# Strassen-like blocks of the down projection: weight sums made in place, and by adding DMAs in two blocks

## The chip, the cores and the metric

One NeuronCore of a Trainium2 chip runs the kernel. The metric is the device time of one execution in microseconds (us), median of 3 runs.

## The reference, cut to what matters

One layer of a diffusion transformer on 256 tokens of width 2048. After attention and a first layer norm, the feed-forward part and the second norm end the layer:

```python
def swiglu(u, w_gate, w_up, w_down):
    return (jax.nn.silu(u @ w_gate) * (u @ w_up)) @ w_down

x = layer_norm(DN_ALPHA * x + g1 * (heads @ w_out[layer]), ln1_g[layer], ln1_b[layer])
x = layer_norm(DN_ALPHA * x + g2 * swiglu(modulate(x, sh2, sc2), w_gate[layer], w_up[layer], w_down[layer]),
               ln2_g[layer], ln2_b[layer])
```

All is float32. Call `h = silu(u @ w_gate) * (u @ w_up)`, 256 x 5632; the change concerns only `h @ w_down`, with `w_down` 5632 x 2048.

## The kernel before, in words

**Precision.** TensorE multiplies float32r numbers. Each float32 operand is split into a rounded part (hi) and the rest (lo), and one product of tiles is three matmuls: hi·hi, lo·hi, hi·lo (`mm3`, L242 to L244). For a weight tile of 128 x 1024, ScalarE casts hi (L232 in `split_raw`, L238 in `split`) and VectorE subtracts to get lo (L233, L239). Four hi and four lo tiles rotate (`HL_BUFS = 4`), so ScalarE and VectorE can be at most four tiles ahead of TensorE.

**The down projection.** The rows of `w_down` are 11 groups f of 512, its columns 4 blocks n of 512, done as two pairs of column blocks (n = 0, 1 and n = 2, 3). For one f and one n, `plain` loads a 512 x 512 piece (1 MB, SP's queue, L210), splits it into two tiles and runs 24 matmuls, all four 128-row chunks for the first 128 tokens and then for the other 128. In a pair, the word "f3" of this text is group 3 with the pair's first column block, "s3" group 3 with its second.

**By quarters.** For some groups (8, 9, 10 in the first pair, 7 to 10 in the second) `by_quarters` does both column blocks of the pair at once. It takes h as 2 x 2 (tokens by row halves) and the weights as 2 x 2 (b11, b12 in one loaded 1 MB tile, b21, b22 in another), and needs 7 products of 6 matmuls in place of 8. Their names, in order: p1, b, a, p7, p5, p6, c. Four of the seven right-hand sides are sums of weights, which VectorE makes with four 128 x 1024 additions (L1780): two into the extra tile `room["x"]` (names x1, x2; "sums" in the trace), two in place. Each product then splits its right side into one hi and one lo tile. Products p1, p5, p6, p7 are collected in four PSUM banks of their own and put together once per pair (`combine_parts`, L1815 to L1820).

The left sums s1 to s4 of a group are made beforehand: `quarter_sums` for 8 to 10 in the first pair, and `late_quarter_sums` for 7, which writes them over quarters of h that nothing reads any more. The one in group 7's own tile can only be written when "s7" is done.

**The order.** Before, the words of the first pair are f0 f1 8 f2 f3 9 f4 f5 f6 f7 s0 10 s1 C s2 s3 A s4 Q s5 s6 s7 R, of the second f0 f1 E 7 f2 8 f3 9 f4 10 f5 f6 s0 C L N s1 A s2, then the last four groups of the last block together. C combines the products, A and E finish a column block (gate, residual, norm statistics), Q and R are the late sums, L loads the rows of the last norm, N makes rows of it (a memset and small DMAs on GpSimd's queue, L1739 and L1741, and an activation on ScalarE, L1743). This part lies outside the hand-ordered regions: a planner lays out each engine's instructions at build time, the program's order being the priority, and an instruction that is not ready by its reckoning can be passed by a later one. Each engine and each queue then runs in that order.

**Raw tiles.** Four 1 MB tiles (`RAW_BUFS = 4`) rotate for the loads. A group by quarters holds two until its last product is split.

Of the kernel before, what the change touches and what calls it, by code (L numbers as in the profile page):

```python
# [16 lines left out]
AF = mybir.ActivationFunctionType  # L17
# [148 lines left out]
def dit_layer(ctx: ExitStack, tc: tile.TileContext, x, c, cx, c_ctx, w_ada, b_ada, w_in, q_norm_g,  # L166
# [37 lines left out]
    def raw_tile():  # L204
        return wraw.tile([P, G4 * NB], F32, tag="raw", name="raw")

    def load_raw(w, k0, nk, c0, width):
        raw = raw_tile()
# [1278 lines left out]
    def quarter_sums(f, hf):  # L1487
        i = list(QUARTERS).index(f)
        if i == 0:
            both = pb.tile([P, 2, 2, 4, 2, P], F32R, tag="u2h", name="quarters")  # L1490
            room["q"] = [both[:, 0], both[:, 1], pb.tile([P, 2, 4, 2, P], F32R, tag="u2l0", name="quarters")]
            room["x"] = pb.tile([P, 2, 2 * NB], F32, tag="u2l1", name="sums")
        hl = [room["q"][i][:, c] for c in range(2)]
        quarters[f] = [[p[:, c] for c in range(4)] for p in hl]
        sums = room["x"][:, 0].rearrange("p (s q t) -> p s q t", s=4, q=2)
        s1, s2, s3, s4 = (sums[:, c].rearrange("p q (a i) -> p q a i", a=4) for c in range(4))
        (a11, a12), (a21, a22) = ([hf[t].rearrange("p (a q i) -> p q a i", a=4, q=Q)[:, k : k + 2] for k in (0, 2)]
                                  for t in range(NT))
        for o, x0, x1, op in ((s1, a21, a22, ALU.add), (s2, s1, a11, ALU.subtract), (s3, a11, a21, ALU.subtract),
                              (s4, a12, s2, ALU.subtract)):  # L1500
            nc.vector.tensor_tensor(o, x0, x1, op=op)
        split(*hl, sums)

    def late_quarter_sums(f):
        whole, sums = (room["x"][:, i] for i in range(2))
        nc.vector.tensor_add(whole, hTh[f].rearrange("p q t -> p (q t)").bitcast(F32), hTl[f].rearrange("p q t -> p (q t)").bitcast(F32))
        whole = whole.rearrange("p (q t) -> p q t", q=4)
        (a11, a12), (a21, a22) = ([whole[:, k : k + 2, t * P : (t + 1) * P] for k in (0, 2)] for t in range(NT))
        sums = sums.rearrange("p (s q t) -> p s q t", s=4, q=2)
        s1, s2, s3, s4 = (sums[:, c] for c in range(4))  # L1510
        quarters[f] = [[c[g][:, 0:2, P:] for g in (f, *QUARTERS)] for c in (hTh, hTl)]
        for o, x0, x1, op in ((s1, a21, a22, ALU.add), (s2, s1, a11, ALU.subtract), (s3, a11, a21, ALU.subtract),
                              (s4, a12, s2, ALU.subtract)):
            nc.vector.tensor_tensor(o, x0, x1, op=op)
# [244 lines left out]
    def by_quarters(f, n, bank, begins, ends, last):
        r1, r2 = (load_raw(w_down, f * 4 + k, 2, n * NB, 2 * NB).rearrange("p (k n) -> p k n", k=2) for k in (0, 2))  # L1760
        (b11, b12), (b21, b22) = ([r[:, :, :NB], r[:, :, NB:]] for r in (r1, r2))
        x1, x2 = (room["x"][:, i].rearrange("p (k n) -> p k n", k=2) for i in range(2))
        h = [(c[f][:, 0:2, :P], c[f][:, 2:4, :P], c[f][:, 2:4, P:]) for c in (hTh, hTl)]
        q = quarters[f]
        lefts = {n: [h[c][i] for c in range(2)] for i, n in enumerate(("a11", "a12", "a22"))}
        lefts.update({f"s{i + 1}": [q[c][i] for c in range(2)] for i in range(4)})
        sub, add = ALU.subtract, ALU.add
        for name, left, right, after in (
            ("p1", "a11", b11, (x1, b22, b12, sub)),
            ("b", "s4", b22, (b12, b12, b11, sub)),  # L1770
            ("a", "a12", b21, (x2, x1, b11, add)),
            ("p7", "s3", x1, (b21, b21, x2, sub)),
            ("p5", "s1", b12, None),
            ("p6", "s2", x2, None),
            ("c", "a22", b21, None),
        ):
# [4 lines left out]
            own = len(name) == 2  # L1781
            for j in range(2):
                mm3(bank(name), lefts[left][0][:, j], lefts[left][1][:, j], (hi[:, j], lo[:, j]),
                    j == 0 and begins(name), j == 1 and (ends if own else last and name != "b"))
        turn()
        turn()

    def pair(n, order, by_parts, left=0):
        banks, begun, held = {}, set(), {}

        def bank(name):
# [9 lines left out]
        whole = [f for f in order if f not in by_parts]
        parts = [f for f in order if f in by_parts]

        def first(f):
            if f in by_parts:
                return lambda: by_quarters(f, n, bank, begins, f == parts[-1], f == order[-1])
            return lambda: plain(f, n, (bank("a"), bank("c")), begins("a") | begins("c"), f == order[-1])

        def second(f):
            return lambda: plain(f, n + 1, (bank("b"), bank("d")), False, f == whole[-1 - left])  # L1810
# [32 lines left out]
    one = pair(0, ORDER, tuple(QUARTERS))
    run(one[0][:-1])
    second_start(0, 1, one[5])
    run(one[0][-1:])
    run(one[1][1:2])
    one[2]()
    run(one[1][2:4])
    one[3]()  # L1850
    run(one[1][4:5])
    rest = late_quarter_sums(LATE_F)
    run(one[1][5:])
    rest()
    two = pair(2, LATE_ORDER, (LATE_F, *QUARTERS), 1)
    run(two[0][:2])
    one[4]()
    run(two[0][2:])
    second_start(0, 3, two[5])
    two[2]()  # L1860
    l2_loads()
    rows_of_last_norm()
    run(two[1][1:2])
    two[3]()
    run(two[1][2:-4])
# [3 lines left out]
    fs = two[6][-4:]  # L1869
# [92 lines left out]
```

## Time and profile before

| | |
|---|---|
| median of 3 runs | 1114.36 us (1113.22 to 1115.82) |
| the profiled execution | 1114.99 us, span 1113.2 us |
| TensorE matmul busy | 1099.1 us |
| VectorE, ScalarE, GpSimd busy | 911.0, 606.9, 46.2 us |
| mean granted TensorE clock | 0.997 of full speed |

The down projection runs from about 870 us to the end. The difference of execution and span lies around the program. A matmul row lasts some 0.39 us, but the matmuls are pipelined: what counts is the distance from one start to the next. In a row of the timeline, a bracket at the end is the idle time before it and what ended it.

### The profile page before, as it was taken

The numbers are of one execution on the slowest core, as the hardware profiler recorded it, in microseconds if no ns is written. First come the engines' busy times: TensorE is split into PE (matmuls) and PEld (weight loads), VectorE is DVE, ScalarE is ACT, GpSimd is POOL, SyncE is SP. The second block draws the span as 40 slices with busy tenths as digits, with TensorE's granted clock in tenths as the row PEclk, the third lists the DMA queues.
The fourth block names the chain that finished last, engine by engine and source line by source line (L and its number), as shares of the span: only waits on it lengthen the run. The fifth ranks groups of instructions, "written<-read, shape, count | busy, mean of one in ns | idle before, by whom it ended". The sixth has DMA issues, their size and how long they took to land.

```text
span 1113.2 us, 13937 instructions
## 1 busy us (share of the span) xinstructions
PE 1099.1 (99%) x5132; PEld 887.0 (80%) x5132; DVE 911.0 (82%) x1098; ACT 606.9 (55%) x875; POOL 46.2 (4%) x94
## 2 busy tenths in 40 slices
PE   8999999999999999999999999999999999999997
PEld 6677788778888778888888888888888778888786
DVE  2469999999999898877666776887875897979996
ACT  3345675786775356444465455655654564446640
POOL 1000050102000010000000000000000000000000
PEclk9999999999999999999999999999999999999999
DMA  9999998889999789989768798898996564646562
GB/s 346 380 400 390 394 335 323 301 274 313 328 313 374 278 311 359 335 293 344 265 208 279 274 339 293 296 316 277 325 322 219 163 249 155 241 175 227 200 254 76
DMA packets 174954, 321.26 MB, mean 289 GB/s; under 512 B 9091, under 2 KB 46883, under 8 KB 172581
## 3 DMA queue, kind: packets, MB, share of 16 engines
q1 hardware_dynamic: 173206, 319.23, 81.6%
q10 hardware_dynamic: 1264, 1.11, 0.3%
q8 instruction: 40, 0.66, 0.2%
q14 instruction: 28, 0.23, 0.1%
q0 software_dynamic: 416, 0.04, 0.0%
HBM read 304.09 MB, written 16.25 MB: 288 GB/s over the span
## 4 chain that ended last, share of the span: by engine, by line
PE 91%; DVE 5%; DMA 3%; ACT 1%; issue 0%; POOL 0%; DVEq 0%; SPq 0%; ACTq 0%
PE acc L242 21%; PE acc L244 21%; PE acc L243 21%; PE wk L243 7%; PE wk L244 7%; PE wk L242 7%; PE wk L1038 2%; PE wk L560 2%; DVE lo L239 2%; DMA raw<-in_w_down_dram 1%; DMA raw<-in_w_ada_dram 1%; DVE raw L1780 1%; PE wk L730 1%; DVE sums L1780 1%; DMA adav<-in_b_ada_dram 0%; DMA rows<-in_ln_g_dram 0%
## 5 line engine op out<-in xcount | busy, mean ns | idle before, releaser
L233 DVE TENSOR_TENSOR lo<-raw,hi 128x1024 fp32r<-128x1024 f32 x228 | 275.4, 1220 | 116.7 <-ACT hi L232 114.3
L232 ACT CAST hi<-raw 128x1024 fp32r<-128x1024 f32 x228 | 239.4, 1055 | 237.1 <-PE acc L244 123.8
L242 PE MATMUL acc<-hi,u2h 128*128 128x512 f32 x448 | 175.1, 391 | 0.0
L244 PE MATMUL acc<-hi,u2l 128*128 128x512 f32 x448 | 174.5, 390 | 0.4 <-DVE u2l L1596 0.4
L243 PE MATMUL acc<-lo,u2h 128*128 128x512 f32 x448 | 174.5, 389 | 0.0
L361 DVE SCALAR_TENSOR_TENSOR adav<-raw,cs,adav 128x1024 f32<-128x1024 f32 (+1 forms) x96 | 114.4, 1191 | 7.2 <-DMA raw<-in_w_ada_dram 3.7
L509 ACT CAST hi<-raw 128x1024 fp32r<-128x1024 f32 x84 | 87.9, 1052 | 54.8 <-PE acc L244 35.8
L512 DVE TENSOR_TENSOR lo<-raw,hi 128x1024 fp32r<-128x1024 f32 x84 | 101.3, 1220 | 9.8 <-ACT hi L509 9.5
L242 PE MATMUL acc<-hi,uh 128*128 128x512 f32 x256 | 102.8, 402 | 0.3 <-ACT uh L743 0.3
L244 PE MATMUL acc<-hi,ul 128*128 128x512 f32 x256 | 100.3, 392 | 0.0
L243 PE MATMUL acc<-lo,uh 128*128 128x512 f32 x256 | 99.8, 390 | 0.0
L244 PE MATMUL wk<-hi,u2l 128*128 128x512 f32 x256 | 99.6, 389 | 0.0
L243 PE MATMUL wk<-lo,u2h 128*128 128x512 f32 x256 | 99.6, 389 | 0.0
L242 PE MATMUL wk<-hi,u2h 128*128 128x512 f32 x256 | 99.6, 389 | 0.0
L242 PE MATMUL acc<-hi,hTh 128*128 128x512 f32 x254 | 98.8, 389 | 0.6 <-ACT hi L238 0.6
L243 PE MATMUL acc<-lo,hTh 128*128 128x512 f32 x254 | 98.8, 389 | 0.0
L244 PE MATMUL acc<-hi,hTl 128*128 128x512 f32 x254 | 98.7, 389 | 0.0
L244 PEld LDWEIGHTS acc<-hi,u2l 128*128 128x128 f32 x448 | 84.1, 188 | 18.3 <-DVE u2l L1596 0.9
L242 PEld LDWEIGHTS acc<-hi,u2h 128*128 128x128 f32 x448 | 84.1, 188 | 18.2 <-ACT u2h L1595 0.8
L243 PEld LDWEIGHTS acc<-lo,u2h 128*128 128x128 f32 x448 | 84.1, 188 | 17.7 <-DVE lo L233 0.4
L242 PEld LDWEIGHTS acc<-hi,uh 128*128 128x128 f32 x256 | 48.1, 188 | 16.1 <-ACT acc L524 2.5
L244 PEld LDWEIGHTS acc<-hi,ul 128*128 128x128 f32 x256 | 48.0, 188 | 11.3 <-DVE ul L746 1.1
(328 smaller groups left out, 1786.1 us busy)
## 6 DMA issues: line engine op xcount, KB each, us to landing
raw<-in_w_ada_dram SPq DMA_DIRECT2D x64, 1024.0 KB, 7.5
raw<-in_w_gate_dram SPq DMA_DIRECT2D x44, 1024.0 KB, 6.4
raw<-in_w_up_dram SPq DMA_DIRECT2D x44, 1024.0 KB, 5.7
raw<-in_w_down_dram SPq DMA_DIRECT2D x44, 1024.0 KB, 5.2
raw<-in_w_ada_dram SPq DMA_DIRECT2D x64, 512.0 KB, 6.3
raw<-in_w_in_dram SPq DMA_DIRECT2D x18, 1024.0 KB, 7.8
raw<-in_w_out_dram SPq DMA_DIRECT2D x16, 1024.0 KB, 6.3
pd<-hx SPq DMA_DIRECT2D x64, 128.0 KB, 5.0
```

What stands on the lines that cost most here:

```text
L232: nc.scalar.copy(hi[:, :n], raw[:, s : s + n])
L233: nc.vector.tensor_tensor(lo[:, :n], raw[:, s : s + n], hi[:, :n].bitcast(F32), op=ALU.subtract)
L239: nc.vector.tensor_tensor(lo, src, hi.bitcast(F32), op=ALU.subtract)
L242: nc.tensor.matmul(ps, lhsT=xh, rhs=w[0], start=first, stop=False, skip_group_check=seeded)
L243: nc.tensor.matmul(ps, lhsT=xh, rhs=w[1], start=False, stop=False, skip_group_check=seeded)
L244: nc.tensor.matmul(ps, lhsT=xl, rhs=w[0], start=False, stop=last, skip_group_check=seeded)
L361: nc.vector.scalar_tensor_tensor(a[:, c : c + piece], raw[:, f : f + piece], cs[:, 4 * (g * (G4 * NB // w) + j) + 2, None], a[:, c : c + p ...
L509: nc.scalar.copy(hl.hi[:, :n], raw.t[:, s : s + n])
L512: nc.vector.tensor_tensor(hl.lo[:, :n], raw.t[:, s : s + n], hl.hi[:, :n].bitcast(F32), op=ALU.subtract)
L560: nc.tensor.matmul(bank.t[32 * j : 32 * j + 32, :width], lhsT=cs[:, 4 * k + 2 - 2 * i : 4 * k + 34 - 2 * i], rhs=raw.t[:, c * width : (c + ...
L1038: nc.tensor.matmul(o_ps.t[:, : 2 * P].rearrange("p (g q) -> p g q", q=32), lhsT=v, rhs=pv[:, k], start=k == 0, stop=k == 3)
L1780: nc.vector.tensor_tensor(after[0], after[1], after[2], op=after[3])
```

## The change

Weight sums no longer use `room["x"]`: all four are made in place, with other signs (b22 += b12, b12 += b11, b11 += b22, b21 += b11), each after the product that reads the old content has split it. The left sums change their signs accordingly, and so do the copy of p1 and one subtraction in `first_block`.

In the second pair the groups 7 and 9 are taken apart into three words each: "a" (loads, p1, b, a, p7, p5), "b" (p6), "c" (product c). In these two groups the last two sums (b11 += b22, b21 += b11; 512 KB each, as 128 partitions of two runs of 2 KB) are made by DMAs from SBUF to SBUF with addition, issued on GpSimd's queue. Groups 8 and 10 of that pair, and all of the first, keep four additions on VectorE.

The four raw tiles are held by hand in the second pair: two are kept for 7 and then 9, the other two and the freed `room["x"]` rotate for all other loads. "s7" moves to the head of the first pair's second half, and R ahead of s6.

```diff
-ORDER = (0, 1, 8, 2, 3, 9, 4, 5, 6, 7, 10)
-LATE_ORDER = (0, 1, 7, 2, 8, 3, 9, 4, 10, 5, 6)
+FIRST_PAIR = "f0 f1 8 f2 f3 9 f4 f5 f6 f7 s7 10 s0 s1 C s2 s3 A s4 Q s5 R s6"
+SECOND_PAIR = "f0 f1 E 7a f2 8 7b f3 7c f4 f5 9a 10 9b f6 9c s0 C L N s1 A s2"
...
+        def product(word, name, left, right):
             hi, lo = (whl.tile([P, SUB * NB], F32R, tag=tag, name=tag).rearrange("p (k n) -> p k n", k=2) for tag in ("hi", "lo"))
-            split(hi, lo, right)
-            if after:
-                nc.vector.tensor_tensor(after[0], after[1], after[2], op=after[3])
+            split(hi, lo, st[right])
...
+        def put_on(right, other):
+            nc.vector.tensor_add(st[right], st[right], st[other])
+
+        def put_apart(right, other):
+            nc.gpsimd.dma_start(st[right], st[other], accum_op=ALU.add)
+
+        last_sum = put_apart if apart else put_on
+
+        def one(word):
+            loads()
+            product(word, "p1", "a11", "b11")
+            product(word, "b", "s4", "b22")
+            put_on("b22", "b12")
+            product(word, "a", "a12", "b21")
+            put_on("b12", "b11")
+            if apart:
+                last_sum("b11", "b22")
+                last_sum("b21", "b11")
+            product(word, "p7", "s3", "b22")
+            if not apart:
+                last_sum("b11", "b22")
+            product(word, "p5", "s1", "b12")
+            if not apart:
+                last_sum("b21", "b11")
+            turn()
+
+        def two(word):
+            product(word, "p6", "s2", "b11")
+
+        def three(word):
+            product(word, "c", "a22", "b21")
+            turn()
...
-            nc.scalar.copy(c1, banks["p1"])
+            nc.scalar.activation(c1, banks["p1"], AF.Copy, scale=-1.0)
...
+    kept = [raw_tile() for _ in range(4)]
+    room["kept"], room["rooms"] = kept[:2], kept[2:] + [room["x"].rearrange("p i n -> p (i n)")]
```

## Rows read from the trace of the kernel before

**Rows 1.** The page: busy time, share of the span and instructions of the engines.

```profile
PE 1099.1 (99%) x5132; PEld 887.0 (80%) x5132; DVE 911.0 (82%) x1098; ACT 606.9 (55%) x875; POOL 46.2 (4%) x94
```

**Rows 2.** The page: the chain that ended last, shares of the span by engine.

```profile
PE 91%; DVE 5%; DMA 3%; ACT 1%; issue 0%; POOL 0%; DVEq 0%; SPq 0%; ACTq 0%
```

**Rows 3.** Windows: stretch, its length, then busy (count) of PE, PEld, DVE, ACT, POOL, clock, DMA share, GB/s.

```profile
860.00:980.00 120.00, 119.04 (x522) 97.27 (x521) 101.93 (x113) 62.31 (x65) 0.00 (x0) 1.00 0.59 204
980.00:1060.00 80.00, 79.39 (x350) 65.09 (x349) 74.93 (x72) 47.38 (x48) 4.40 (x8) 1.00 0.57 200
```

**Rows 4.** Timeline of PE: start, length, engine, line, operation, out<-in.

```profile
885.81 0.40 PE L243 MATMUL wk<-lo,quarters 128*128 128x512 f32 x1
...
887.74 0.50 PE L242 MATMUL acc<-hi,hTh 128*128 128x512 f32 x1 [0.61 <-ACT hi L238]
...
908.81 0.50 PE L243 MATMUL wk<-lo,quarters 128*128 128x512 f32 x1 [0.29 <-DVE lo L239]
...
1041.79 0.39 PE L244 MATMUL acc<-hi,hTl 128*128 128x512 f32 x1
...
1043.38 0.39 PE L242 MATMUL wk<-hi,hTh 128*128 128x512 f32 x1
...
1049.09 0.40 PE L242 MATMUL wk<-hi,quarters 128*128 128x512 f32 x1
1050.10 0.50 PE L243 MATMUL wk<-lo,quarters 128*128 128x512 f32 x1 [0.61 <-DVE lo L239]
1050.44 0.40 PE L244 MATMUL wk<-hi,quarters 128*128 128x512 f32 x1
```

**Rows 5.** Timeline of DVE around block 10 of the second pair.

```profile
1037.82 1.22 DVE L1745 SCALAR_TENSOR_TENSOR rows<-rows 1x1024 fp32r<-1x1024 f32 x1
1039.06 1.23 DVE L239 TENSOR_TENSOR lo<-raw,hi 128x1024 fp32r<-128x1024 f32 x1
1040.20 1.22 DVE L1780 TENSOR_TENSOR sums<-raw 128x1024 f32<-128x1024 f32 x1
...
1046.55 1.23 DVE L239 TENSOR_TENSOR lo<-sums,hi 128x1024 fp32r<-128x1024 f32 x1 [0.59 <-ACT hi L238]
...
1048.83 1.22 DVE L239 TENSOR_TENSOR lo<-raw,hi 128x1024 fp32r<-128x1024 f32 x1
```

**Rows 6.** Timeline of ACT: casts beside plain groups, and in block 10 of the second pair.

```profile
953.82 1.06 ACT L232 CAST hi<-raw 128x1024 fp32r<-128x1024 f32 x1 [3.02 <-PE acc L244]
955.18 1.06 ACT L232 CAST hi<-raw 128x1024 fp32r<-128x1024 f32 x1 [0.30 <-PE acc L244]
959.26 1.06 ACT L232 CAST hi<-raw 128x1024 fp32r<-128x1024 f32 x1 [3.02 <-PE acc L244]
...
1038.61 1.05 ACT L238 CAST hi<-raw 128x1024 fp32r<-128x1024 f32 x1 [0.77 <-DMA raw<-in_w_down_dram]
1042.22 1.06 ACT L238 CAST hi<-raw 128x1024 fp32r<-128x1024 f32 x1 [2.56 <-PE acc L244]
1044.95 0.63 ACT L1743 ACTIVATE rows<-rows 65x512 fp32r<-65x512 f32 x1 [1.68 <-DMA rows<-in_ln_g_dram]
```

**Rows 7.** Timeline of DVE ahead of block 10 of the first pair: sums made early.

```profile
926.24 1.23 DVE L1780 TENSOR_TENSOR sums<-raw 128x1024 f32<-128x1024 f32 x1
...
928.65 1.22 DVE L1780 TENSOR_TENSOR sums<-sums,raw 128x1024 f32<-128x1024 f32 x1
```

**Rows 8.** DMA issues by line: out<-in queue, count, KB each, median us to landing.

```profile
raw<-in_w_down_dram SPq DMA_DIRECT2D x44, 1024.0 KB, 5.2
raw<-in_w_ada_dram SPq DMA_DIRECT2D x64, 512.0 KB, 6.3
...
spill<-hd SPq DMA_DIRECT2D x20, 256.0 KB, 8.1
...
rows<-in_ln_g_dram POOLq DMA_DIRECT2D x3, 4.0 KB, 5.0
```

**Rows 9.** Timeline of GpSimd in the second pair: the only DMAs it issues there.

```profile
1039.03 1.44 POOL L1741 DMA_DIRECT2D rows<-in_ln_g_dram  x3 [0.29 <-POOL rows L1739]
```

More of the change, by code (lines that the diff above doesn't have):

```diff
@@ L205, in raw_tile, with load_raw @@
         return wraw.tile([P, G4 * NB], F32, tag="raw", name="raw")
-    def load_raw(w, k0, nk, c0, width):
-        raw = raw_tile()
+    def load_raw(w, k0, nk, c0, width, raw=None):
+        raw = raw_tile() if raw is None else raw
         rv = raw[:, : nk * width]
@@ L1498, in quarter_sums @@
                                   for t in range(NT))
-        for o, x0, x1, op in ((s1, a21, a22, ALU.add), (s2, s1, a11, ALU.subtract), (s3, a11, a21, ALU.subtract),
-                              (s4, a12, s2, ALU.subtract)):
-            nc.vector.tensor_tensor(o, x0, x1, op=op)
+        for o, x0, x1 in ((s1, a21, a22), (s2, a11, s1), (s3, a21, a11), (s4, a12, s2)):
+            nc.vector.tensor_sub(o, x0, x1)
         split(*hl, sums)
@@ L1511, in late_quarter_sums @@
         quarters[f] = [[c[g][:, 0:2, P:] for g in (f, *QUARTERS)] for c in (hTh, hTl)]
-        for o, x0, x1, op in ((s1, a21, a22, ALU.add), (s2, s1, a11, ALU.subtract), (s3, a11, a21, ALU.subtract),
-                              (s4, a12, s2, ALU.subtract)):
-            nc.vector.tensor_tensor(o, x0, x1, op=op)
+        for o, x0, x1 in ((s1, a21, a22), (s2, a11, s1), (s3, a21, a11), (s4, a12, s2)):
+            nc.vector.tensor_sub(o, x0, x1)
         def put_in(i):
@@ L1751, in mms, with plain_room @@
             mm3(ps, hTh[f][:, j, tt], hTl[f][:, j, tt], w[j], first and j == 0, last and j == 3)
+    def plain_room():
+        if "rooms" not in room:
+            return None
+        room["rooms"].append(room["rooms"].pop(0))
+        return room["rooms"][-1]
     def plain(f, n, accs, begins, ends):
-        w = load_split(w_down, f * 4, n * NB)
+        w = split_raw(load_raw(w_down, f * 4, G4, n * NB, NB, plain_room()))
         for t in range(NT):
-            mms(f, w, t, accs[t], begins, ends)
+            mms(f, w, t, accs[t], begins, ends[t] if isinstance(ends, tuple) else ends)
@@ L1757, in plain, with by_quarters, loads @@
         turn()
[L1759 to L1776, printed above, removed]
+    def by_quarters(f, n, bank, begins, closes, apart):
+        st = {}
+        def loads():
+            rooms = room["kept"] if apart else [plain_room(), plain_room()]
+            r1, r2 = (load_raw(w_down, f * 4 + k, 2, n * NB, 2 * NB, r).rearrange("p (k n) -> p k n", k=2)
+                      for k, r in zip((0, 2), rooms))
+            for i, r in enumerate((r1, r2)):
+                for j in range(2):
+                    st[f"b{i + 1}{j + 1}"] = r[:, :, j * NB : (j + 1) * NB]
+            h = [(c[f][:, 0:2, :P], c[f][:, 2:4, :P], c[f][:, 2:4, P:]) for c in (hTh, hTl)]
+            st.update({a: [h[c][i] for c in range(2)] for i, a in enumerate(("a11", "a12", "a22"))})
+            st.update({f"s{i + 1}": [quarters[f][c][i] for c in range(2)] for i in range(4)})
+        def product(word, name, left, right):
@@ L1777, in by_quarters @@
             hi, lo = (whl.tile([P, SUB * NB], F32R, tag=tag, name=tag).rearrange("p (k n) -> p k n", k=2) for tag in ("hi", "lo"))
-            split(hi, lo, right)
-            if after:
-                nc.vector.tensor_tensor(after[0], after[1], after[2], op=after[3])
-            own = len(name) == 2
+            split(hi, lo, st[right])
             for j in range(2):
-                mm3(bank(name), lefts[left][0][:, j], lefts[left][1][:, j], (hi[:, j], lo[:, j]),
-                    j == 0 and begins(name), j == 1 and (ends if own else last and name != "b"))
@@ L1785, in by_quarters @@
-        turn()
-        turn()
-    def pair(n, order, by_parts, left=0):
+                mm3(bank(name), st[left][0][:, j], st[left][1][:, j], (hi[:, j], lo[:, j]),
+                    j == 0 and begins(name), j == 1 and closes(word, name))
+        def put_on(right, other):
[3 more added lines that the diff above has]
+        last_sum = put_apart if apart else put_on
@@ L1789, in pair @@
+        def two(word):
[3 more added lines that the diff above has]
+            turn()
+        return one, two, three
+    def pair(n, words, left=0):
         banks, begun, held = {}, set(), {}
@@ L1799, in begins, with used, closes, step @@
             return fresh
[L1801 to L1810, printed above, removed]
+        words = words.split()
+        seconds = [int(w[1:]) for w in words if w[0] == "s"]
+        uses = {"f": ("a", "c"), "s": (), "1": ("p1", "b", "a", "p7", "p5"), "2": ("p6",), "3": ("c",)}
+        def used(word):
+            if word[0] in uses and not word[0].isdigit():
+                return uses[word[0]]
+            if not word[0].isdigit():
+                return ()
+            kind = {"a": "1", "b": "2", "c": "3"}.get(word[-1], "123")
+            return tuple(b for k in kind for b in uses[k])
+        last = {b: w for w in words for b in used(w)}
+        def closes(word, name):
+            return name != "b" and last[name] == word
+        def step(word):
+            if word[0] == "f":
+                f = int(word[1:])
+                return lambda: plain(f, n, (bank("a"), bank("c")), begins("a") | begins("c"), tuple(last[b] == word for b in "ac"))
+            if word[0] == "s":
+                f = int(word[1:])
+                if f == seconds[0]:
+                    return lambda: second_start(f, n + 1, bank)
+                return lambda: plain(f, n + 1, (bank("b"), bank("d")), False, f == seconds[-1] and not left)
+            if word[0].isdigit():
+                f = int(word.rstrip("abc"))
+                if f not in parted:
+                    parted[f] = by_quarters(f, n, bank, begins, closes, word[-1] == "a")
+                one, two, three = parted[f]
+                return lambda: [q(word) for q in {"a": (one,), "b": (two,), "c": (three,)}.get(word[-1], (one, two, three))]
+            return {"C": combine_parts, "A": first_block}[word]
+        parted = {}
         def combine_parts():
@@ L1825, in first_block @@
                 y = held[t]
-                nc.vector.tensor_add(y, banks["ac"[t]], y)
+                nc.vector.tensor_sub(y, banks["ac"[t]], y)
                 gated(t, n, y, y)
@@ L1833, in second_block @@
                 spread(t, n + 1)
-        return [first(f) for f in order], [second(f) for f in whole], combine_parts, first_block, second_block, bank, whole
+        return [step(w) if w not in extra else extra[w] for w in words], second_block, bank
     def second_start(f, n, bank):
-        w = load_split(w_down, f * 4, n * NB)
+        w = split_raw(load_raw(w_down, f * 4, G4, n * NB, NB, plain_room()))
         mms(f, w, 0, bank("b"), False, False)
@@ L1841, in second_start @@
         turn()
[L1843 to L1865, printed above, removed]
+    rest = []
+    extra = {
+        "Q": lambda: rest.append(late_quarter_sums(LATE_F)),
+        "R": lambda: rest[0](),
+        "L": l2_loads,
+        "N": rows_of_last_norm,
+    }
+    one, one_end, _ = pair(0, FIRST_PAIR)
+    run(one)
+    kept = [raw_tile() for _ in range(4)]
+    room["kept"], room["rooms"] = kept[:2], kept[2:] + [room["x"].rearrange("p i n -> p (i n)")]
+    extra["E"] = one_end
+    two, _, two_bank = pair(2, SECOND_PAIR, 1)
+    run(two)
     wide = pb.tile([P, 2, 2, SUB * NB], F32R, tag="u2h", name="wide")
@@ L1868, in dit_layer @@
     cols = [slice(n * NB, (n + 1) * NB) for n in range(4)]
-    fs = two[6][-4:]
+    fs = LAST_F
     ws = [load_split(w_down, f * 4, 3 * NB, rooms=() if i else wide) for i, f in enumerate(fs[:3])]
@@ L1878, in dit_layer @@
         for f, w in zip(fs[:3], ws):
-            mms(f, w, t, two[5]("bd"[t]), False, f == fs[2])
+            mms(f, w, t, two_bank("bd"[t]), False, f == fs[2])
         mms(fs[3], ws[3], t, ends[t], True, True)
@@ L1890, in dit_layer @@
             nc.vector.tensor_mul(scaled[n], xt[:, 1, cols[n]], l2g[:, cols[n]])
-        gated(0, 3, two[5]("b"), t2k("yt"))
+        gated(0, 3, two_bank("b"), t2k("yt"))
         nc.vector.tensor_add(xt[:, 0, cols[3]], xt[:, 0, cols[3]], ends[0])
@@ L1894, in dit_layer @@
         ending(0)
-        gated(1, 3, two[5]("d"), t2k("yt"))
+        gated(1, 3, two_bank("d"), t2k("yt"))
         nc.vector.tensor_add(xt[:, 1, cols[3]], xt[:, 1, cols[3]], ends[1])
```

1 line of the change is left out of this document (added).

## The prediction

> **What bounds the kernel now.** I read the page's engine line first: TensorE is busy 1099.1 of 1113.2 us [rows 1], and the chain that ended last runs on it for 91% of the span [rows 2]. The windows of the down projection show the second candidate: from 980 to 1060 VectorE is busy 74.9 of 80 us, at full clock [rows 3]. Because matmuls overlap in the pipeline, busy time hides small losses, so I then read the starts in the timeline of TensorE. From 1041.79 to 1043.38 there are seven steps: 0.227 us each [rows 4]. So a product (6 matmuls) takes 1.36, a plain group (24) 5.45, a whole block by quarters (42) 9.53 us. Between 860 and 1103 eleven starts come over 0.06 us later than this pitch, the first at 885.81, the last at 1050.44 [rows 4]. Together they lose 3.16 us: 1.47 in or just behind block 8 and 0.56 in block 9 of the first pair, 1.13 in block 10 of the second. The matmuls stay 1:1 the same, so 3.16 us is all that the change can win, and what VectorE saves counts only there.
>
> VectorE starts an operation of 1024 columns every 1.14 us (1039.06 to 1040.20) [rows 5]. A block by quarters costs it seven lo subtractions and four sums, 11 x 1.14 = 12.5 us against TensorE's 9.5. A plain group gives back 5.45 - 2 x 1.14 = 3.2. So block and plain in turn are just balanced: 14.8 against 15.0.
>
> How far VectorE may run ahead is set by the four hi and lo tiles. Beside plain groups the casts lie 1.36 apart, then 4.08 [rows 6]: a plain group's first tile is free after three quarters of it, its second at its end. Call B the moment when a block's first matmul starts (1043.38 in block 10 [rows 4]). Behind a plain group the cast of p1 may start at about B-6.5, of b at B-5.1, of a at B-1.1 (1042.22 [rows 6]), of p7 at B+0.3, then one every 1.36.
>
> **The change part by part.**
>
> *Additions that leave VectorE.* Two in block 7 and two in 9 of the second pair: 4 x 1.14 = 4.6 us. With TensorE as the bound this is worth only stall that it removes. Block 10's stall before is lo of p5, which ended at 1048.83 + 1.22 = 1050.05, and TensorE went on at 1050.10 [rows 4, 5]. In front of it stood an operation for the last norm's row (1.22 us) and a wait of 0.59 behind ScalarE's wait for that row's DMA [rows 5, 6]. N's second row now hangs on 9c and falls beside plain groups. So these 1.13 us go: -1.1.
>
> *Sums in place, the block behind a plain group.* Before, a sum into x could be made before any tile was free (926.24 to 928.65, some 12 us ahead of its products [rows 7]). In place, each sum must wait until the old content is split. By the cast times above, VectorE ends p1 at B-4.2, b at -2.8, two sums at -1.7 and -0.5, a at 1.3, p7 2.6, a sum 3.8, p5 4.9, a sum 6.0, p6 7.2, c 8.3. TensorE wants lo one matmul into each product: p7 at 4.3, p5 5.7, p6 7.0, c 8.4. So p6 is late by 0.2. That is +0.2 for block 8 of the second pair and +0.2 for block 10 of the first, which had no stall. Blocks 8 and 9 of the first pair begin with VectorE or their load late; eleven operations from the same start end at the same time, so 0.
>
> *9a straight ahead of 10.* This is the new squeeze. 9a has no plain group behind it; block 10's tiles become free one product at a time. With S the start of 9a, B = S+6.8. The cast of p1 may start only when 9's b is through: B-3.8; b B-2.4, a B-1.1. VectorE then ends p1 at B-1.5, b -0.1, sum 1.0, a 2.2, sum 3.3, p7 4.5, sum 5.6, p5 6.7, sum 7.9, p6 9.0, c 10.2. Against the same wants p7 is late by 0.2, p5 by 1.1 in all, p6 by 2.0, c by no more. The last operation alone gives 10.2 - 8.4 = 1.8 as the least; a planner that holds sums back behind the splits changes little. What could hide it is a longer lead, and four tiles allow none. +2.0. After 7a comes f2, so block 8 is spared.
>
> *The adding DMAs.* The trace shows none. For 9, the second sum on VectorE is done by about S-1, so the first DMA can start there; b's split needs the tile free at S+12.3 and is wanted at S+16.3. The second DMA needs the first landed, and 9c is wanted at S+6.8+9.5+1.4+5.4 = S+23.1. With X per DMA and 2.3 for cast and lo, 9c is in time while -1 + 2X + 2.3 is below 23.1: X up to 10.9. 7 has more room (f3 starts later): X up to 13.6. Bounds of X: 5.0, the landing of 4 KB that GpSimd issues; above, 2 x 8.1 = 16.2, the slowest small transfer with DRAM taken twice because an add also reads its target. I take 6.3, a 512 KB load with the same bytes [rows 8]; the chain of two is then 12.6 and costs 0. Both ends stay for the range. The Trainium skill ("DMA: Bandwidth & Descriptors", Anatomy of one DMA) prices such a DMA at 2.0 us plus bytes at 436 GB/s, by estimate 3.2 us here; no row shows it, and by it the chain would never be late. Traffic: 2 MB of adds in some 90 us beside DMA engines busy 57% [rows 3]. Loads have five rooms instead of four, and today's waits for them are short (0.77 [rows 6]): 0, at worst +1.
>
> *GpSimd's queue.* Issuing three small DMAs took 1.44 us [rows 9] and nothing urgent stands there: the adds of 9 and the memsets and DMAs of N, needed only in the last norm. 0.
>
> *Rest.* Copy of p1 with a scale, subtraction for addition: same operations. s7 first and R earlier end a wait that was off the path. The rooms: k0, k1 for block 9 are free when 7c is split, some 16 us ahead of 9a, against 5.2 us for a load [rows 8]. 0.
>
> Sum: -1.1 + 0.2 + 0.2 + 2.0 = +1.3 us. Against the profiled execution, 1114.99, that is 1116.3; it stands 0.6 above the median, 1114.36, so for a median I say 1115.6.
>
> **The rivals.**
>
> *The squeeze does not form.* The planner may order block 10's sums, casts and matmuls so that 9b or f6 fills the gap, or the model above is too strict by one tile. Then -1.1 +0.4 at most remains: 1113.3; and if the freer in-place sums also end the first pair's 2.0, 1111.2. For it: 4.6 us less work on VectorE. Against: eleven operations per block stay in 8 and 10 and in the whole first pair.
>
> *The adds come late (slower).* One mechanism: the chain of two DMAs of block 9 ends behind the moment when 9c wants it, ScalarE waits there in order, and s0's casts behind it. It decides from X = 10.9. At X = 12.6 (6.3 twice) it costs 2 x 1.7 = 3.4: 1119.0. At 16.2 it costs 10.6, and 7c 5.2 more: 1131. For it: GpSimd's 4 KB take 5.0 already, and the add reads twice. Against: 512 KB loads at 6.3.
>
> *The issue is held up.* VectorE is without a pause through 9a and 10, some 17 us. If GpSimd could not write its descriptors then, the chain of 9 would start at S+16 and 9c be late by about 6 us net of the squeeze: 1121. Against: the three issues at 1039.03 took 1.44 us while VectorE ran back to back [rows 5, 9]. The Trainium skill ("SBUF — State Buffer", Summary) says that descriptor writing starves while VectorE is in a doubled mode; 1024 columns in 1.14 us are no doubled rate, so by that rule and the trace it should not.
>
> *It does what it says and nothing shows:* the saved additions lie off the path, squeeze of 0.5 to 1: 1114.4. This I count with the forecast.
>
> **How the numbers follow.** 0.2% is 2.2 us: about what a measurement of this kernel tells from no change. Forecast with its neighbours, 1114.2 to 1117.2: 0.60, of which 0.09 lies above 1116.6. No squeeze: 0.24, of which 0.08 below 1112.1. Adds late: 0.13, all slower. Issue held up: 0.03, slower. So faster 0.08, same 0.67, slower 0.25. The range, 1112.4 to 1118.8, leaves out most of the fast end of the one rival and the late adds beyond X = 12.
>
> **What would show it.** In the changed profile: TensorE's starts inside block 10 of the second pair late by 1.5 to 2.5 us in sum, with VectorE's lo as releaser and no VectorE pause from 9a to 9b; no late start at 7b, 7c, 9b, 9c; the two adds of a block landing within some 13 us of each other's issue; N's operations beside plain groups. Wrong would be: a stall at 9c released by a DMA; no stall in block 10; or first-pair stalls that are not again 1.5 to 2.3 us.

## The result: slower by half a per cent

The changed kernel takes 1119.58 us (median of 6 runs, 1118.42 to 1121.0) against 1114.05 us: ratio 1.005, 95% interval 1.0037 to 1.0063. The sign was the one forecast; the size, +5.5 us, lies outside the range given (1115.6, from 1112.4 to 1118.8). The profiled execution took 1119.22 us, its span 1117.4.

The windows of the changed kernel, columns as in [rows 3]; the last line is the third window of the kernel before:

```profile
860.00:980.00 120.00, 117.80 (x515) 95.78 (x514) 102.14 (x114) 61.37 (x65) 0.00 (x0) 1.00 0.61 210
980.00:1060.00 80.00, 78.71 (x345) 64.21 (x344) 67.81 (x60) 45.24 (x44) 7.44 (x8) 1.00 0.60 183
1060.00:1103.00 43.00, 41.14 (x181) 33.37 (x180) 39.51 (x55) 16.34 (x17) 2.05 (x4) 1.00 0.53 199
...
1060.00:1103.00 43.00, 43.00 (x191) 35.63 (x190) 38.34 (x52) 14.51 (x15) 0.00 (x0) 1.00 0.46 166
```

VectorE did get less to do: 67.8 us in place of 74.9 between 980 and 1060. The clock is the full one in all three. And yet TensorE has less busy time in each of the stretches. The late starts on TensorE, counted as before against the pitch of 0.227 us, say where (timeline of the changed kernel; L243 to L245 are the three matmuls of a product):

```profile
886.00 0.50 PE L243 MATMUL wk<-hi,quarters 128*128 128x512 f32 x1 [0.37 <-ACT hi L239]
...
888.27 0.50 PE L243 MATMUL acc<-hi,hTh 128*128 128x512 f32 x1 [0.62 <-ACT hi L239]
...
889.21 0.50 PE L243 MATMUL acc<-hi,hTh 128*128 128x512 f32 x1 [0.45 <-ACT hi L233]
...
912.53 0.51 PE L244 MATMUL acc<-lo,hTh 128*128 128x512 f32 x1 [0.38 <-DVE lo L240]
...
1046.84 0.39 PE L243 MATMUL wk<-hi,hTh 128*128 128x512 f32 x1
...
1053.64 0.50 PE L243 MATMUL wk<-hi,quarters 128*128 128x512 f32 x1 [0.63 <-ACT hi L239]
...
1055.91 0.50 PE L243 MATMUL acc<-hi,hTh 128*128 128x512 f32 x1 [0.61 <-ACT hi L239]
...
1079.75 0.50 PE L244 MATMUL acc<-lo,hTh 128*128 128x512 f32 x1 [1.78 <-DVE lo L234]
...
1081.49 0.50 PE L244 MATMUL acc<-lo,hTh 128*128 128x512 f32 x1
```

Three places lose 8.26 us in sum, where before two pairs lost 3.16 [rows 4]: the first pair 3.70 (before 2.03), block 10 of the second pair 2.14 (before 1.13), and a new place behind it, in the plain word s2, 2.42 (before nothing). That is 5.1 of the 5.5 us.

**The third place** is read off three engines. GpSimd may clear the tile of the last norm's second row only when 9c is through, and then issues the small DMAs:

```profile
1046.23 1.22 POOL L1789 DMA_DIRECT2D raw<-raw  x1 [4.58 <-DVE lo L240]
1066.93 0.52 POOL L1738 MEMSET rows<- 65x512 f32 x1 [19.49 <-PE acc L245]
1067.76 1.53 POOL L1740 DMA_DIRECT2D rows<-in_ln_g_dram  x3 [0.31 <-POOL rows L1738]
```

ScalarE stands before the row's activation until they land, while TensorE is in s1, with a weight cast queued behind it:

```profile
1070.98 1.06 ACT L233 CAST hi<-raw 128x1024 fp32r<-128x1024 f32 x1 [1.25 <-PE acc L245]
1074.71 0.63 ACT L1742 ACTIVATE rows<-rows 65x512 fp32r<-65x512 f32 x1 [2.68 <-DMA rows<-in_ln_g_dram]
1075.25 1.04 ACT L233 CAST hi<-raw 128x1024 fp32r<-128x1024 f32 x1
```

VectorE stands idle for 3.01 us too, because the row's operation comes next on its queue, and the work of A is behind that:

```profile
1071.69 0.68 DVE L1157 TENSOR_TENSOR xt<-xt,v 128x512 f32<-128x512 f32 x1
1075.38 0.68 DVE L1744 SCALAR_TENSOR_TENSOR rows<-rows 1x512 fp32r<-1x512 f32 x1 [3.01 <-ACT rows L1742]
...
1077.88 0.67 DVE L1156 TENSOR_TENSOR u<-u,adav 128x512 f32<-128x512 f32 x1
1078.48 1.22 DVE L234 TENSOR_TENSOR lo<-raw,hi 128x1024 fp32r<-128x1024 f32 x1
```

That last lo ends at 1079.70, and TensorE goes on at 1079.75.

**Block 10 of the second pair** is the squeeze, and the trace follows the forecast's ledger almost to the tenth. With B = 1046.84 (the fence above), it gave the ends p1 -1.5, b -0.1, sum 1.0, a 2.2, sum 3.3, p7 4.5, sum 5.6, p5 6.7, sum 7.9, p6 9.0. Start plus length here gives -1.5, -0.2, 1.0, 2.2, 3.3, 4.5, 5.6, 6.7, 7.9, 9.0 (VectorE, all of block 10; "sums" is the freed extra tile, now a raw tile):

```profile
1044.09 1.23 DVE L240 TENSOR_TENSOR lo<-sums,hi 128x1024 fp32r<-128x1024 f32 x1
1045.40 1.23 DVE L240 TENSOR_TENSOR lo<-raw,hi 128x1024 fp32r<-128x1024 f32 x1
1046.66 1.22 DVE L1786 TENSOR_TENSOR raw<-raw,sums 128x1024 f32<-128x1024 f32 x1
1047.81 1.22 DVE L240 TENSOR_TENSOR lo<-raw,hi 128x1024 fp32r<-128x1024 f32 x1
1048.94 1.22 DVE L1786 TENSOR_TENSOR sums<-sums 128x1024 f32<-128x1024 f32 x1
1050.08 1.22 DVE L240 TENSOR_TENSOR lo<-raw,hi 128x1024 fp32r<-128x1024 f32 x1
1051.21 1.22 DVE L1786 TENSOR_TENSOR sums<-sums,raw 128x1024 f32<-128x1024 f32 x1
1052.35 1.22 DVE L240 TENSOR_TENSOR lo<-sums,hi 128x1024 fp32r<-128x1024 f32 x1
1053.48 1.22 DVE L1786 TENSOR_TENSOR raw<-raw,sums 128x1024 f32<-128x1024 f32 x1
1054.62 1.22 DVE L240 TENSOR_TENSOR lo<-sums,hi 128x1024 fp32r<-128x1024 f32 x1
```

The lo of p7, p5 and p6 end at 1051.30, 1053.57 and 1055.84 here, and TensorE's late starts are at 1051.35, 1053.64 and 1055.91. Counted from B, these are the second matmuls of the three products, which read lo. The names and the releaser (ScalarE's hi) that the rows at 1053.64 and 1055.91 carry don't fit this count; the second of them would put the first matmul of product c ahead of the rest of p6. By the count and the times, lo is what TensorE waited for; the names alone don't show it.

**The first pair.** In block 8 VectorE now does three small sums for the left side of group 9 (L1501) between the block's last weight sum and its last two lo:

```profile
885.84 1.22 DVE L1786 TENSOR_TENSOR raw<-raw 128x1024 f32<-128x1024 f32 x1
886.97 0.42 DVE L1501 TENSOR_TENSOR sums<-spill,sums 128x256 f32<-128x256 f32 x1
887.31 0.42 DVE L1501 TENSOR_TENSOR sums<-spill 128x256 f32<-128x256 f32 x1
887.64 0.42 DVE L1501 TENSOR_TENSOR sums<-spill,sums 128x256 f32<-128x256 f32 x1
887.98 2.35 DVE L240 TENSOR_TENSOR lo<-raw,hi 128x1024 fp32r<-128x1024 f32 x2
```

Before, they came behind the block. The diff has the reason, though not in the sums: `turn()`, which releases the next group's prepared steps, stood twice at a block's end and now stands once in `one`, ahead of p6 and c.

**The adding DMAs** were never waited for. Three of the four land 5.0 us after their issue, the second one of group 7 after 9.4 (columns as in [rows 8], with the median). The second of block 9 was issued at 1046.23 (GpSimd's fence above); the cast for product c starts at 1058.74, after the last cast of f6:

```profile
raw<-raw POOLq DMA_DIRECT2D x4, 512.0 KB, 5.0
...
rows<-in_ln_g_dram POOLq DMA_DIRECT2D x3, 2.0 KB, 5.8
```

### The profile page after: what moved, and what is told of

It is laid out like the page before. It is cut to its first block, busy times and chain, and to the rows that moved or that the text cites. A ratio compares the mean times of both kernels' runs of the same rounds, so it can differ in the third digit from the quotient of the medians.

```text
span 1117.4 us, 13949 instructions
## 1 busy us (share of the span) xinstructions
PE 1100.4 (98%) x5132; PEld 887.4 (79%) x5132; DVE 909.0 (81%) x1094; ACT 606.3 (54%) x875; POOL 51.1 (5%) x98
## 3 DMA queue, kind: packets, MB, share of 16 engines
q0 software_dynamic: 1504, 2.14, 1.1%
## 4 chain that ended last, share of the span: by engine, by line
PE 89%; DVE 4%; issue 2%; DMA 2%; ACT 1%; SPq 0%; POOL 0%; DVEq 0%; ACTq 0%; POOLq 0%
PE acc L243 21%; PE acc L245 21%; PE acc L244 21%; PE wk L243 7%; PE wk L245 7%; PE wk L244 7%; PE wk L1039 2%; PE wk L561 2%; DVE lo L240 1%; DMA raw<-in_w_ada_dram 1%; DVE raw L1786 1%; PE wk L731 1%; DMA rows<-in_ln_g_dram 1%; DMA adav<-in_b_ada_dram 0%; DVE lo L234 0%
## 5 line engine op out<-in xcount | busy, mean ns | idle before, releaser
L234 DVE TENSOR_TENSOR lo<-raw,hi 128x1024 fp32r<-128x1024 f32 x222 | 268.3, 1221 | 123.4 <-ACT hi L233 121.8
L233 ACT CAST hi<-raw 128x1024 fp32r<-128x1024 f32 x222 | 232.2, 1054 | 233.8 <-PE acc L245 126.8
L243 PE MATMUL acc<-hi,u2h 128*128 128x512 f32 x448 | 175.1, 391 | 0.0
L245 PE MATMUL acc<-hi,u2l 128*128 128x512 f32 x448 | 174.5, 390 | 0.5 <-DVE u2l L1595 0.5
L510 ACT CAST hi<-raw 128x1024 fp32r<-128x1024 f32 x84 | 87.9, 1052 | 57.0 <-PE acc L245 29.4
L513 DVE TENSOR_TENSOR lo<-raw,hi 128x1024 fp32r<-128x1024 f32 x84 | 101.3, 1221 | 10.7 <-ACT hi L510 10.5
L243 PE MATMUL acc<-hi,uh 128*128 128x512 f32 x256 | 102.8, 402 | 0.3 <-ACT uh L744 0.3
L243 PE MATMUL acc<-hi,hTh 128*128 128x512 f32 x254 | 99.0, 390 | 1.7 <-ACT hi L239 1.2
L245 PE MATMUL acc<-hi,ul 128*128 128x512 f32 x256 | 100.3, 392 | 0.0
L245 PE MATMUL wk<-hi,u2l 128*128 128x512 f32 x256 | 99.6, 389 | 0.0
L243 PE MATMUL wk<-hi,u2h 128*128 128x512 f32 x256 | 99.6, 389 | 0.0
L245 PE MATMUL acc<-hi,hTl 128*128 128x512 f32 x254 | 98.9, 389 | 0.0
L245 PEld LDWEIGHTS acc<-hi,u2l 128*128 128x128 f32 x448 | 84.1, 188 | 18.5 <-DVE u2l L1595 0.9
L243 PEld LDWEIGHTS acc<-hi,u2h 128*128 128x128 f32 x448 | 84.1, 188 | 18.1 <-ACT u2h L1594 0.8
L239 ACT CAST hi<-raw 128x1024 fp32r<-128x1024 f32 x46 | 48.1, 1053 | 42.5 <-PE acc L245 28.2
L240 DVE TENSOR_TENSOR lo<-raw,hi 128x1024 fp32r<-128x1024 f32 x46 | 55.4, 1220 | 7.7 <-ACT hi L239 6.5
```

The costliest lines, as they stand in the source:

```text
L233: nc.scalar.copy(hi[:, :n], raw[:, s : s + n])
L234: nc.vector.tensor_tensor(lo[:, :n], raw[:, s : s + n], hi[:, :n].bitcast(F32), op=ALU.subtract)
L239: nc.scalar.copy(hi, src)
L240: nc.vector.tensor_tensor(lo, src, hi.bitcast(F32), op=ALU.subtract)
L243: nc.tensor.matmul(ps, lhsT=xh, rhs=w[0], start=first, stop=False, skip_group_check=seeded)
L245: nc.tensor.matmul(ps, lhsT=xl, rhs=w[0], start=False, stop=last, skip_group_check=seeded)
```

## The experiments

In the table the lost time of a kernel is the sum of TensorE's late starts in its profile, worked out as above; the ratio is to the kernel before, on the same chip. The kernel before had medians of 1113.9 to 1114.3 us in the sets of runs, so medians of different sets compare to within about 0.4 us. Set by set the kernels are: before and changed; e1 to e4; e6 to e10; e11 to e13.

| kernel | first pair | second, to block 10 | behind | lost, us | median, us | ratio, interval |
|---|---|---|---|---|---|---|
| before | 2.03 | 1.13 | 0 | 3.16 | 1114.05 | |
| changed | 3.70 | 2.14 | 2.42 | 8.26 | 1119.6 | 1.005 (1.0037 to 1.0063) |
| e1 | 3.68 | 2.56 | 0 | 6.24 | 1117.9 | 1.0034 (1.0021 to 1.0048) |
| e2 | 2.02 | 2.09 | 2.40 | 6.51 | 1117.8 | 1.0028 (1.0017 to 1.0039) |
| e3 | 3.73 | 0.82 | 0.92 | 5.47 | 1116.4 | 1.0019 (1.0010 to 1.0027) |
| e4 | 2.48 | 1.53 | 0 | 4.01 | 1115.3 | 1.001 (1.0001 to 1.0019) |
| e6 | 3.73 | 3.28 | 2.14 | 9.15 | 1120.9 | 1.0062 (1.0049 to 1.0074) |
| e8 | 3.71 | 2.11 | 0.73 | 6.55 | 1117.7 | 1.0034 (1.0021 to 1.0046) |
| e9 | 2.04 | 0 | 0.47 | 2.51 | 1113.9 | 0.9999 (0.9990 to 1.0008) |
| e10 | 1.48 | 0 | 0 | 1.48 | 1112.2 | 0.9981 (0.9972 to 0.9990) |
| e11 | 2.05 | 0.82 | 0.75 | 3.62 | 1115.8 | 1.0018 (1.0009 to 1.0027) |
| e12 | 1.12 | 0 | 0 | 1.12 | 1111.8 | 0.9984 (0.9975 to 0.9992) |
| e13 | 0.33 | 0 | 0 | 0.33 | 1111.3 | 0.9976 (0.9968 to 0.9985) |

Median less lost time is 1110.6 to 1112.2 us in every row: the late starts of the down projection are what the thirteen kernels differ in, to within about 0.8 us.

**e1: the second row into other tiles.** Group 7's tiles are free after 7c.

```diff
-        for i, (f, n) in enumerate(((8, 2), (9, 1))):
+        for i, (f, n) in enumerate(((8, 2), (7, 1))):
```

> The changed kernel, but the second row of the last norm is put into the tiles of group 7 (free after 7c) and no longer into those of group 9 (free only after 9c). Theory: the 2.4 us lost at the second-pair word s2 (late starts from 1079.75 to 1081.83) is the wait of ScalarE, and of VectorE behind it, for that row's DMA of 5.8 us, so it goes: 1117.2 us by the median of the changed kernel (1119.6), 2.4 us less, no late start after 1070. Rival (C's and A's work on VectorE is simply too much beside s0, s1, s2): the wait at s2 stays at over 1.5 us and the time at 1118.5 to 1120. Other rival: the wait moves with the row to where it now stands (between f5 and 9's casts) and costs there: time within 1 us of 1119.6.

The late starts behind block 10 are gone, all 2.42 us; 0.4 came back in block 10. So the theory holds for the place it speaks of, and 0.6 us of the forecast gain didn't come. The second rival is right in part: ScalarE now waits 1.53 us for that row's DMA at 1035.96, between the first two casts of 9a.

**e2: both turns at the end of a whole block.**

```diff
                 last_sum("b21", "b11")
-            turn()
+            if apart:
+                turn()
...
             product(word, "c", "a22", "b21")
             turn()
+            if not apart:
+                turn()
```

> The changed kernel, but in a block that is not taken apart the two turns that release the next group's prepared steps both come at its end again, as before the change. Theory: the first pair loses 3.7 us in place of 2.0 because the first turn, now in mid-block, lets the four small sums of the next group's left side in between the block's own weight sums on VectorE; with the turns at the end it loses 2.0 to 2.3, and the time falls by 1.4 to 1.7 us, to about 1118.0. Rival (sums in place are what costs the first pair, 11 operations with a later start): the first pair still loses over 3.2 us, time 1119 to 1120.

As the theory said: the first pair loses 2.02 us, and the kernel gains 1.7. VectorE's order in block 8 of this kernel, p6's lo now ahead of the small sums:

```profile
886.04 1.22 DVE L1786 TENSOR_TENSOR raw<-raw 128x1024 f32<-128x1024 f32 x1
887.17 1.22 DVE L240 TENSOR_TENSOR lo<-raw,hi 128x1024 fp32r<-128x1024 f32 x1
888.31 0.42 DVE L1501 TENSOR_TENSOR sums<-spill,sums 128x256 f32<-128x256 f32 x1
888.64 1.22 DVE L240 TENSOR_TENSOR lo<-raw,hi 128x1024 fp32r<-128x1024 f32 x1
```

That 2.02 so nearly equals the 2.03 of before is chance. Of those 2.03 us, 0.56 followed a load that landed late in that one execution (see e10); the 1.48 us of e10, the same program up to there, are without it. Against that, e2 loses 0.33 us more in block 8, as long as the one small sum (0.34) that still stands ahead of the block's first weight sum, at 878.89, and 0.24 us in block 9. Whether the sums in place have a part in these 0.5 us no run separates.

**e3: a plain group between 9a and 10.**

```diff
-SECOND_PAIR = "... f3 7c f4 f5 9a 10 9b f6 9c ..."
+SECOND_PAIR = "... f3 7c f4 9a f5 10 9b f6 9c ..."
```

> The changed kernel, but the words f5 and 9a change places, so that a plain group stands between 9a and 10. Theory of the squeeze (as predicted, 2.0 us): the 2.1 us lost in block 10 of the second pair fall to about 0.2, time 1117.7. Rival (VectorE's eleven operations in a block are too many wherever it stands, or the adding DMAs slow it): block 10 still loses over 1.2 us, time above 1118.6.

Block 10 loses nothing any more: the squeeze is shown. The 0.82 left stand ahead of it, in 9a, where ScalarE now waits 1.48 us for the first row's DMA. That the place at s2 fell from 2.42 to 0.92 was not foreseen. VectorE's queue shows how: the planner has put two of A's operations ahead of the row's, so VectorE waits 1.10 us there in place of 3.01:

```profile
1071.77 0.69 DVE L1157 TENSOR_TENSOR xt<-xt,c 128x512 f32<-128x512 f32 x1
1072.37 0.68 DVE L1883 TENSOR_TENSOR u<-acc,u 128x512 f32<-128x512 f32 x1
1074.15 0.68 DVE L1744 SCALAR_TENSOR_TENSOR rows<-rows 1x512 fp32r<-1x512 f32 x1 [1.10 <-ACT rows L1742]
```

**e4: the three edits together.**

> All three edits of the other kernels of this set in one. Theory (three separate causes that add up): late starts of 2.2 to 2.5 us in the whole down projection, nearly all in the first pair; 5.5 to 6.2 us less than the changed kernel, 1113.5 to 1114.1 us, the same as before the change or up to 0.8 us less. Rival (one shared cause, such as too little slack on VectorE or slower loads beside the adding DMAs): the gains don't add up, time 1116 or more.

A miss: 1115.3. At s2 nothing is lost any more, but the row's wait is back in a new place, in 9a. There and in f5 behind it 0.98 us are lost, in block 10 another 0.55; the first pair loses 0.46 more than in e2, with a wait of 0.73 us for block 9's load on ScalarE. With the row in group 7's tile its wait now stands between the first two casts of 9a, where the words are tight (ScalarE):

```profile
1032.56 1.06 ACT L239 CAST hi<-raw 128x1024 fp32r<-128x1024 f32 x1 [0.93 <-PE acc L245]
1035.70 0.63 ACT L1742 ACTIVATE rows<-rows 65x512 fp32r<-65x512 f32 x1 [2.08 <-DMA rows<-in_ln_g_dram]
1036.24 1.99 ACT L239 CAST hi<-raw 128x1024 fp32r<-128x1024 f32 x2
```

So the activation stands in ScalarE's order ahead of the moment when the row's DMA lands, 5.3 us after its issue here. That the planner reckons with a shorter landing is likely, and not shown. Moving the row is no cure; the wait itself had to go.

**e8: the rows without DMAs of their own.** L loads the same vector, broadcast to all partitions, and the activation can read it there. That load moves up to stand behind f1.

```diff
-            raw = pb.tile([P, 2, NB], F32, tag=f"hTl{f}", name="rows")[:, :n, :]
...
-            nc.gpsimd.memset(raw[: 2 * 32 + 1], 0.0)
-            for p in range(0, 3 * 32, 32):
-                nc.gpsimd.dma_start(raw[p : p + 1], ...)
+            raw = late["l2"][0][:, 2 * i * NB : (2 * i + n) * NB].rearrange("p (k n) -> p k n", n=NB)
```

> The changed kernel, but the rows of the last norm are made from the broadcast row tile that L loads anyway (its first load stands at the start of the pair's program), so that the memsets and the six small DMAs on GpSimd's queue go; the tiles of groups 8 and 9 stay. Theory (the 2.4 us at s2 are the wait for the small DMA, not the work of ScalarE and VectorE on the row): they go, and the operation of 1.2 us now also done there costs 0 to 0.5: 1117.2 to 1117.7. Rival (the work of C, A and the rows beside s0 to s2 is too much): at least 1.5 us stay lost there, 1118.7 or more.

2.42 fell to 0.73, although both rows' operations now stand at this place: the wait was the larger part, the crowd of operations the rest. The time is at the upper end of the theory's.

**e9: e2, e3 and e8 in one.**

> The turns at the block's end, a plain group between 9a and 10, and the rows from the broadcast tile, in one kernel. Theory: the first pair loses 2.0 to 2.4 us, the second 0 to 0.3, since no wait for a small DMA is left on ScalarE: 1113.3 to 1114.0 us, up to 0.8 us less than before the change. Rival (moving the words costs more elsewhere): as the kernel with the three edits before, 1115.3.

1113.9, as the theory said, and the same as before the change: the three edits take back the whole loss. But one of them, the rows' edit, also removes a wait that the kernel before had itself; e10 is the fair kernel to compare with.

**e10: the kernel before, with e8's edit alone.** The same edit of the rows.

> The kernel before, with the rows of the last norm made from the broadcast row tile and no small DMAs, nothing else changed. Theory (the 1.13 us lost in block 10 of the second pair before are the row's operation and ScalarE's wait for its DMA): they go, 1112.9 to 1113.4 us. Rival (they are VectorE's eleven operations per block): block 10 keeps at least 0.7 us, and the time stays at 1114.1.

1112.2, faster than the kernel before, and more than forecast: block 10 loses nothing. VectorE's eleven operations per block were no bound there; the row's wait was. On ScalarE both rows now follow the casts of the plain groups and wait for nothing:

```profile
1058.56 1.06 ACT L232 CAST hi<-raw 128x1024 fp32r<-128x1024 f32 x1 [0.30 <-PE acc L244]
1059.52 1.57 ACT L1738 ACTIVATE rows<-l 65x1024 fp32r<-65x1024 f32 x2
1062.64 1.06 ACT L232 CAST hi<-raw 128x1024 fp32r<-128x1024 f32 x1 [1.55 <-PE acc L244]
```

That block 9 of the first pair doesn't lose its 0.56 us in this profile has another reason than the edit. In the kernel before, a load of that block took 7.8 us to land, and ScalarE and VectorE waited 0.64 and 0.89 us for it; here the same load took 6.4 us and neither waited. ScalarE's cast, before and then here:

```profile
897.83 1.05 ACT L238 CAST hi<-raw 128x1024 fp32r<-128x1024 f32 x1 [0.64 <-DMA raw<-in_w_down_dram]
...
898.08 1.06 ACT L238 CAST hi<-raw 128x1024 fp32r<-128x1024 f32 x1 [0.26 <-PE acc L244]
```

So the edit accounts for 1.13 us of the gain; how often that load comes late is not known from one profile.

With the same rows, the change is still behind: e9 takes 1.7 us more than e10, in the same set of runs, and loses 1.0 us more by late starts, 0.56 in the first pair and 0.47 in s2. So with its three causes of loss removed, the change is still not faster than the kernel before, and slower than that kernel with the same edit.

**e6 and e11: no adding DMAs.** In the changed kernel (e6) and in e9 (e11), VectorE makes the four sums.

```diff
         def put_apart(right, other):
-            nc.gpsimd.dma_start(st[right], st[other], accum_op=ALU.add)
+            nc.vector.tensor_add(st[right], st[right], st[other])
```

> The changed kernel, but the last two sums of groups 7 and 9 are made by VectorE at the same places in the program, and by no DMA. Theory (VectorE's queue is what decides in 9a and 10): two more operations of 1.14 us stand ahead of block 10, whose loss grows from 2.1 to about 4.4 us; groups 7 and 8 have slack, 0 to 0.5 us; the rest as in the changed kernel: 1121.5 to 1122.5 us. Rival (the adding DMAs themselves cost, through contention or through their landing): taking them out gains or changes nothing, 1119.6 us or less.

> As the kernel with turns at the block's end, a plain group between 9a and 10, and rows from the broadcast tile (1113.9 us), but the last two sums of groups 7 and 9 on VectorE and no adding DMAs. Theory (with a plain group between the blocks VectorE's lead covers the two additions): second pair loses 0 to 0.5 us, time 1113.9 to 1114.4. Rival (the DMAs are what keeps the second pair free of loss): 1 to 2 us more, 1114.9 to 1116.

e6 is slower than the changed kernel by 1.3 us, right in sign, half in size: block 10 and its neighbours lose 1.1 more, not 2.3. The intervals of the two overlap, so the time alone doesn't tell. e11 is a miss on the other side: 1.8 us slower than e9, 1.1 of it seen as late starts (0.82 in groups 7 to 10, 0.28 behind). A plain group doesn't cover the two additions. So the adding DMAs are a gain of 1.3 to 1.8 us over VectorE's additions, and the rival that they harm on balance has fallen.

**e12 and e13: e10 with block 8 of the first pair later.**

```diff
-ORDER = (0, 1, 8, 2, 3, 9, 4, 5, 6, 7, 10)
+ORDER = (0, 1, 2, 8, 3, 4, 9, 5, 6, 7, 10)   # e12
+ORDER = (0, 1, 2, 3, 8, 4, 9, 5, 6, 7, 10)   # e13
```

> The kernel before with rows from the broadcast tile (1112.2 us, loses 1.48 us in and behind block 8 of the first pair), and in the first pair the words f0 f1 f2 8 f3 f4 9 f5 f6 f7 in place of f0 f1 8 f2 f3 9 f4 f5 f6 f7. Theory (block 8 starts when VectorE still has the last gate and the left sums to do; a plain group more gives it 3.2 us of lead): the 1.48 us fall to 0 to 0.4, time 1110.8 to 1111.4. Rival (the block's eleven operations lose it wherever the block stands): 1112.0 to 1112.6.

> As the last one, with block 8 another plain group later: f0 f1 f2 f3 8 f4 9 f5 f6 f7. Theory: nothing more to win in block 8, but only f4 between 8 and 9 and the left sums of 10 to be placed: 0 to 0.6 us more than with the order f0 f1 f2 8 f3 f4 9. Rival (one plain group isn't lead enough for block 8): 0.4 to 1 us less.

e12's time, 1111.8, lies between its theory and its rival. One plain group more was not enough (0.89 us still lost in block 8), two were; e13's theory was wrong, its rival right. e13 is the fastest of all: 1111.3 us, 0.9976 of the kernel before (0.9968 to 0.9985), with 0.33 us lost in the whole down projection and without any of the change. Among e10, e12 and e13 the intervals overlap; what tells them apart is the late starts, 1.48, 1.12 and 0.33 us.

## Why the prediction was right in sign and wrong in size

Its sum was -1.1 + 0.2 + 0.2 + 2.0 = +1.3. By its own steps:

- *"9a straight ahead of 10": +2.0.* Right, in mechanism and size: 2.14 in block 10, gone with a plain group between (e3), and the ledger matches the trace.
- *"N's second row now hangs on 9c and falls beside plain groups. So these 1.13 us go."* This step failed. The 1.13 left block 10, but the wait behind them did not go, it moved and grew to 2.42, because beside s1 and s2 the work of C and A is queued on VectorE behind it. The rows of before had shown the mechanism (1.68 us on ScalarE for that DMA [rows 6]); I priced its cover as free without looking at what is queued beside the plain groups there. e1, e4 and e8 show it. Size of the error: 2.4 us.
- *"Blocks 8 and 9 of the first pair ...: eleven operations from the same start end at the same time, so 0."* This failed too, by 1.7 us. The moved `turn()` let three small sums in between, and a step that is moved was not followed in the diff; e2 takes back 1.68. That eleven operations alone would cost 0 is not shown by e2: its agreement with before is chance, and up to 0.5 us stay open. The prediction had named "first-pair stalls that are not again 1.5 to 2.3 us" as a sign of being wrong, and 3.70 came.
- *Block 10 of the first pair: +0.2, block 8 of the second: +0.2.* Not seen: neither shows a late start.
- *The adding DMAs: X of 6.3, cost 0.* X was 5.0 three times, the lower bound taken from GpSimd's 4 KB, and 9.4 once, within the 10.9 and 13.6 that the prediction allowed; the cost is 0, and more than that, a gain of 1.3 to 1.8 us over VectorE's additions (e6, e11). By the Trainium skill ("DMA: Bandwidth & Descriptors", Anatomy of one DMA), 2.0 us plus bytes at 436 GB/s, 512 KB would take 3.2 us, an estimate; the measured 5.0 and 9.4 decide.
- *The issue is held up:* no. A 512 KB add kept GpSimd for 1.22 us while VectorE had hardly a pause. The Trainium skill ("SBUF — State Buffer", Summary) ties the starving of descriptor writing to VectorE's 2x and 4x modes; the additions here, 1024 columns in 1.14 us, I read as neither. By that rule the issue should not be held up, and this trace agrees.
- *Readings.* Before, twelve starts come late and not eleven, the first at 885.47; the sum is the same to 0.02. In the rival without a squeeze, 1113.3 leaves out its own +0.4: 1113.7.

With the two failed steps put right the sum is +1.3 + 2.4 + 1.7 - 0.4 = +5.0, against 5.5 measured. That the time came out near the 1119.0 of the rival "the adds come late" is chance: nothing waited for an add, and 9c has no late start.

## What to carry to other kernels

When an engine runs its queue in order, a small DMA in front of it costs whatever stands behind it: price a moved wait by what is queued at its new place, and rather remove the wait (read data that is loaded anyway) than move it. Where work is taken apart into steps, look at every hook that sits between them, not only at the arithmetic. And before taking work off a busy engine, find which single wait makes its late starts: here one edit of a dozen lines (e10, 0.9981 of the time before) did more than the change with its three causes of loss removed (e9, 0.9999). When a loss seems to be gone or equal, compare what ended each wait in the two profiles: a load that lands 1.4 us later looks like an effect of the edit.

## What the runs showed of the hardware

- A DMA that adds 512 KB from SBUF into SBUF landed 5.0 us after its issue three times and 9.4 us once in the changed kernel, and kept GpSimd for 1.2 us. The slow one is the second add of group 7, with 9.4 to 9.8 us in all seven kernels that have it; why is not shown. 2 KB from DRAM by the same queue took 5.8 us in the same execution: 256 times the bytes took no longer, though the two differ in source too, so the price of the adding itself isn't separated.
- TensorE's granted clock stayed at its upper level, 2.4 GHz, through all these stalls, the longest of them 1.9 us: 1.00 in each window above.
